# Thirty rows of one block's load moved to GpSimd's queue, over fifteen of the sixteen DMA engines

## The chip, the cores and the metric

The kernel runs on one core of one Trainium2 chip. The time is the device time of one execution in microseconds (us), the median of several runs; the span, a little shorter, is from the first to the last instruction of the profiled run. For a program on one core, a run over 1.5% above the fastest of its own kernel counts as slow.

## The reference

```python
# x: 16 x 2048 x 256, W: 256 x 256, lora_A: 256 x 16, lora_B: 16 x 256, m: 256, all float32
W_adapted = W + scale * (lora_A @ lora_B)
W_norm = np.sqrt(np.sum(W_adapted ** 2, axis=0, keepdims=True) + 1e-8)
W_final = W_adapted / W_norm * m
y = x.reshape(-1, 256) @ W_final
```

33.5 MB of x are read and 33.5 MB of y written; the weights are small.

## The kernel before

x is cut into 8 blocks of 4 MB. A block is a tile of 128 partitions with 32 KB ("a row") each. SyncE issues all loads, ScalarE all stores, each over all 128 partitions. Five block buffers hold x, and the result y is written back over it, so the load of block b + 5 waits for the store of block b. Only the last block is loaded and stored in two parts.

```python
XBUFS = 5
parts = [(b * CH, CH) for b in range(NBLK - 1)]
parts += [(NCH - CH, CH // 2), (NCH - CH // 2, CH // 2)]

def in_dram(dram, g0, cnt):
    return dram[g0 * J * P : (g0 + cnt) * J * P].rearrange("(p j) k -> p j k", p=P)

def load_x(n):
    nc.sync.dma_start(
        out=in_sbuf(*parts[n]), in_=in_dram(x_flat, *parts[n])
    ).then_inc(sem(f"load{n}"), 16)
# ... (W on SyncE; A, B and m on ScalarE)
for n in range(len(parts)):
    b = parts[n][0] // CH
    if b >= XBUFS and parts[n][0] % CH == 0:
        nc.sync.wait_ge(sem(f"store{b - XBUFS}"), 16)
    load_x(n)
# ... GpSimd, for every pair p of 4 KB column groups:
    if p == 0 or part_of[2 * p - 1] != part_of[2 * p]:
        nc.gpsimd.wait_ge(sem(f"load{part_of[2 * p]}"), 16)
    nc.gpsimd.tensor_copy(out=xb_bufs[p % NXB][:], in_=x_bufs[...])   # to bf16
# ... TensorE transposes and multiplies, VectorE and ScalarE empty PSUM, ScalarE stores
```

## Time and profile before

| | before |
|---|---|
| time, median of 3 runs | 164.03 us (163.66 to 164.14) |
| span of the profiled run | 163.2 us |
| bytes moved, mean rate | 67.41 MB, 413 GB/s |
| packets of 32 KB (one row) | 1.213 us each, load or store |
| ends of the last store on the 16 DMA engines | 159.8 to 160.7 us for fifteen, 163.2 for one |

### The profile page before, as it was taken

The numbers are of one execution on the slowest core, as the hardware profiler recorded it, in microseconds if no ns is written. First come the engines' busy times: TensorE is split into PE (matmuls) and PEld (weight loads), VectorE is DVE, ScalarE is ACT, GpSimd is POOL, SyncE is SP. The second block draws the span as 40 slices with busy tenths as digits, with TensorE's granted clock in tenths as the row PEclk, the third lists the DMA queues.
The fourth block names the chain that finished last, engine by engine and source line by source line (L and its number), as shares of the span: only waits on it lengthen the run. The fifth ranks groups of instructions, "written<-read, shape, count | busy, mean of one in ns | idle before, by whom it ended". The sixth has DMA issues, their size and how long they took to land. (4 is left out here: it accounts for less than half of the span.)

```text
span 163.2 us, 1988 instructions
## 1 busy us (share of the span) xinstructions
PE 105.3 (65%) x786; PEld 85.2 (52%) x786; DVE 47.2 (29%) x44; ACT 63.8 (39%) x67; POOL 62.5 (38%) x39
## 2 busy tenths in 40 slices
PE   1270599789789897898981998619988820892000
PEld 0130577677577775776760867418676610771000
DVE  0429452350532514405230325005051400330000
ACT  3010027548366384473754053900738440062000
POOL 1006381753935738268004940069209003900000
PEclk9999999999999999999998589985899996599755
DMA  5998998998999999999999999999999999998991
GB/s 201 402 498 386 426 474 385 482 418 265 466 426 426 442 410 466 426 394 482 418 426 442 420 426 458 402 458 410 446 414 454 414 446 422 450 442 377 442 430 60
DMA packets 2915, 67.41 MB, mean 413 GB/s; under 512 B 465, under 2 KB 482, under 8 KB 610
## 3 DMA queue, kind: packets, MB, share of 16 engines
q1 hardware_dynamic: 1440, 33.82, 49.0%
q10 hardware_dynamic: 1474, 33.59, 47.8%
q14 instruction: 1, 0.01, 0.0%
HBM read 33.85 MB, written 33.55 MB: 413 GB/s over the span
## 5 line engine op out<-in xcount | busy, mean ns | idle before, releaser
L219 ACT COPY x_sb<-y_ps 128x1024 f32<-128x1024 f32 x64 | 61.9, 1014 | 75.8 <-PE y_ps L281 75.8
L165 POOL CAST xb<-x_sb 128x2048 bf16<-128x2048 f32 x32 | 60.0, 1902 | 79.3 <-DMA x_sb<-in_x_dram 56.0
L281 PE MATMUL y_ps<-w_final,xt 128*128 128x256 bf16 x512 | 64.6, 280 | 12.8 <-PEq L256 12.8
L202 DVE COPY xt<-xt_ps 128x1024 f32<-128x1024 f32 x32 | 38.2, 1221 | 88.1 <-PE xt_ps L267 88.0
L281 PEld LDWEIGHTS y_ps<-w_final,xt 128*128 128x128 bf16 x512 | 48.4, 100 | 28.2 <-issue 19.8
L267 PE MATMUL xt_ps<-identity,xb 128*128 128x128 f32 x264 | 39.1, 309 | 23.1 <-PEq L256 23.1
L267 PEld LDWEIGHTS xt_ps<-identity,xb 128*128 128x128 f32 x264 | 34.9, 161 | 25.8 <-issue 25.6
L198 DVE TENSOR_TENSOR w_final<-wam,rnorm 128x256 bf16<-128x256 f32 x2 | 4.0, 2028 | 0.0
L244 PE MATMUL y_ps<-sq,ones 128*128 128x256 f32 x4 | 2.1, 674 | 1.6 <-DVE sq L187 1.6
L233 PE MATMUL y_ps<-identity,a_nat 128*16 128x128 f32 x2 | 0.6, 397 | 3.6 <-DMA a_nat<-in_lora_A_dram 3.6
L212 ACT ACTIVATE norm<-y_ps,eps_col 128x256 f32<-128x256 f32 x1 | 0.5, 473 | 6.1 <-PE y_ps L244 6.1
L244 PEld LDWEIGHTS y_ps<-sq,ones 128*128 128x128 f32 x4 | 1.2, 323 | 2.3 <-DVE sq L187 2.1
L210 ACT ACT_TABLE_LOAD x1 | 1.3, 1283 | 2.4 <-issue 2.4
L233 PEld LDWEIGHTS y_ps<-identity,a_nat 128*16 128x16 f32 x2 | 0.1, 90 | 3.6 <-issue 3.6
L171 POOL MEMSET xb<- 128x2048 bf16 x1 | 1.8, 1805 | 0.3 <-PE xt_ps L267 0.3
L195 DVE RECIPROCAL rnorm<-norm 128x256 f32<-128x256 f32 x1 | 1.7, 1745 | 0.0
L237 PE MATMUL y_ps<-b_bf,aT 16*128 16x256 bf16 x2 | 0.6, 404 | 1.5 <-DVE aT L180 1.5
L189 DVE COPY m_all<-y_ps 128x256 f32<-128x256 f32 x1 | 0.4, 425 | 3.3 <-PE y_ps L249 3.3
L178 DVE CAST b_bf<-b_nat 16x256 bf16<-16x256 f32 x1 | 0.3, 281 | 3.8 <-DMA b_nat<-in_lora_B_dram 3.8
L249 PE MATMUL y_ps<-m_row,ones 1*128 1x256 f32 x2 | 1.2, 710 | 0.0
L237 PEld LDWEIGHTS y_ps<-b_bf,aT 16*128 16x128 bf16 x2 | 0.1, 106 | 1.9 <-DVE aT L180 1.9
L183 DVE SCALAR_TENSOR_TENSOR wa<-y_ps,w_nat 128x512 f32<-128x512 f32 x1 | 0.7, 692 | 0.8 <-PE y_ps L237 0.8
(13 smaller groups left out, 3.7 us busy)
## 6 DMA issues: line engine op xcount, KB each, us to landing
x_sb<-in_x_dram SPq DMA_DIRECT2D x7, 4096.0 KB, 27.1
out_dram<-x_sb ACTq DMA_DIRECT2D x7, 4096.0 KB, 37.2
x_sb<-in_x_dram SPq DMA_DIRECT2D x2, 2048.0 KB, 29.6
out_dram<-x_sb ACTq DMA_DIRECT2D x2, 2048.0 KB, 20.2
w_nat<-in_W_dram SPq DMA_DIRECT2D x1, 256.0 KB, 2.9
a_nat<-in_lora_A_dram ACTq DMA_DIRECT2D x1, 16.0 KB, 2.6
b_nat<-in_lora_B_dram ACTq DMA_DIRECT2D x1, 16.0 KB, 3.6
m_row<-in_m_dram ACTq DMA_DIRECT2D x1, 1.0 KB
```

The costliest lines, as they stand in the source:

```text
L165: nc.gpsimd.tensor_copy(out=xb_bufs[p % NXB][:], in_=x_bufs[b % XBUFS][:, 2 * c * J : 2 * (c + 1) * J, :],).then_inc(sem("rounded"), 1)
L171: nc.gpsimd.memset(xb_bufs[NPR % NXB][:], 0.0).then_inc(sem("rounded"), 1)
L183: nc.vector.scalar_tensor_tensor(out=wa[:], in0=ab_ps, scalar=float(scale), in1=w_nat[:], op0=ALU.mult, op1=ALU.add).then_inc(dv, 1)
L195: nc.vector.reciprocal(out=rnorm[:], in_=norm[:]).then_inc(dv, 1)
L198: i = nc.vector.tensor_mul(out=w_final[:, t], in0=wam[:, t], in1=rnorm[:])
L202: nc.vector.tensor_copy(out=xt_bufs[p % NXT][:].rearrange("p r t -> p (r t)").bitcast(FP32), in_=xt_ps[p % 2][:],).then_inc(sem("copied"), 1)
L210: nc.scalar.activation(out=warm[:], in_=eps_col[:], func=AF.Sqrt)
L219: nc.scalar.copy(out=x_bufs[b % XBUFS][:, c * J : (c + 1) * J, :], in_=y_ps[g % 2][:]).then_inc(sem("room"), 1)
L244: i = nc.tensor.matmul(n2_ps, ones[:], sq[:, t, :], start=(t == 0), stop=(t == KC - 1))
L249: nc.tensor.matmul(mb_ps, ones[0:1, :], m_row[:], start=True, stop=True).then_inc(pe, 1)
L267: i = nc.tensor.transpose(xt_ps[p % 2][:, j * P : (j + 1) * P], xb_bufs[p % NXB][:, j, :].bitcast(FP32), identity[:],)
L281: i = nc.tensor.matmul(y_ps[h][:, j, :], xt_bufs[p % NXT][:, r : r + P, t], w_final[:, t, :], start=(t == 0 and (j % (J // 2)) == 0), stop ...
```

## The change

One of the sixteen DMA engines ends 2.5 us after the rest (marks at 160.7 and 163.2 us). The change wants to take two rows of 32 KB off it. It puts 30 rows on GpSimd's queue, means them for fifteen engines, and sends six rows of B ahead of them so that the one left out is the slow one (`SLOW = 5`). Rows 30 and 31 of block 1 go out from SyncE in pieces of 1 KB, the other 96 as one transfer.

```diff
+    SLOW = 5
+    SIDE = 30
+    n_side = next(n for n, (g0, _) in enumerate(parts) if g0 == CH)     # block 1
+    def by_gpsimd(out, in_, name, size):
+        nc.gpsimd.dma_start(
+            out=out, in_=in_, max_dma_last_dim=size, single_packet=True
+        ).then_inc(sem(name), 16)
+
+    def side_loads():
+        dst, src = in_sbuf(CH, CH), in_dram(x_flat, CH, CH)
+        half = DJ * IN * 2
+        by_gpsimd(b_nat[0 : SLOW + 1], lora_B[0 : SLOW + 1], "load_b0", OUT * 2)
+        by_gpsimd(dst[0:SIDE], src[0:SIDE], "side", half)
+        by_gpsimd(b_nat[SLOW + 1 : R], lora_B[SLOW + 1 : R], "load_b1", OUT * 2)
+
     def load_x(n):
+        dst, src = in_sbuf(*parts[n]), in_dram(x_flat, *parts[n])
+        p0 = 0
+        if n == n_side:
+            for p0 in range(SIDE, 32):
+                for s in range(2):
+                    nc.sync.dma_start(
+                        out=dst[p0 : p0 + 1].rearrange("p (j s) k -> p s j k", s=2)[:, s],
+                        in_=src[p0 : p0 + 1].rearrange("p (j s) k -> p s j k", s=2)[:, s],
+                    ).then_inc(sem(f"rows{p0}_{s}"), 16)
+            p0 = 32
+        nc.sync.dma_start(out=dst[p0:P], in_=src[p0:P]).then_inc(sem(f"load{n}"), 16)
...
-    nc.scalar.dma_start(out=b_nat[:], in_=lora_B).then_inc(sem("load_b"), 16)
...
+    side_loads()                       # ahead of GpSimd's first memset
```

(Cut: GpSimd's waits for the five parts of block 1, and VectorE's for the two parts of B.)

More of the change, by code (lines that the diff above doesn't have):

```diff
@@ L120, in in_dram, with wait_x @@
         return dram[g0 * J * P : (g0 + cnt) * J * P].rearrange("(p j) k -> p j k", p=P)
-    def load_x(n):
-        nc.sync.dma_start(
-            out=in_sbuf(*parts[n]), in_=in_dram(x_flat, *parts[n])
-        ).then_inc(sem(f"load{n}"), 16)
+    SLOW = 5
+    SIDE = 30
+    n_side = next(n for n, (g0, _) in enumerate(parts) if g0 == CH)
+    assert parts[n_side] == (CH, CH)
+    def by_gpsimd(out, in_, name, size):
[8 more added lines that the diff above has]
+        by_gpsimd(b_nat[SLOW + 1 : R], lora_B[SLOW + 1 : R], "load_b1", OUT * 2)
+    def load_x(n):
+        dst, src = in_sbuf(*parts[n]), in_dram(x_flat, *parts[n])
[9 more added lines that the diff above has]
+        nc.sync.dma_start(out=dst[p0:P], in_=src[p0:P]).then_inc(sem(f"load{n}"), 16)
+    def wait_x(n):
+        nc.gpsimd.wait_ge(sem(f"load{n}"), 16)
+        if n == n_side:
+            nc.gpsimd.wait_ge(sem("side"), 16)
+            for p0 in range(SIDE, 32):
+                for s in range(2):
+                    nc.gpsimd.wait_ge(sem(f"rows{p0}_{s}"), 16)
     def store_y(n):
@@ L161 @@
         if p == 0 or part_of[2 * p - 1] != part_of[2 * p]:
-            nc.gpsimd.wait_ge(sem(f"load{part_of[2 * p]}"), 16)
+            wait_x(part_of[2 * p])
         if p >= NXB:
@@ L176 @@
     nc.vector.memset(eps_col[:], 1e-8).then_inc(dv, 1)
-    nc.vector.wait_ge(sem("load_b"), 16)
+    nc.vector.wait_ge(sem("load_b0"), 16)
+    nc.vector.wait_ge(sem("load_b1"), 16)
     nc.vector.tensor_copy(out=b_bf[:], in_=b_nat[:])
```

## The prediction

> **What bounds the kernel now.** I read the page's slices first, then windows over the end of the span, then the chain that ended last, then SyncE's waits, and last the head.
>
> ```profile
> DMA  5998998998999999999999999999999999998991
> GB/s 201 402 498 386 426 474 385 482 418 265 466 426 426 442 410 466 426 394 482 418 426 442 420 426 458 402 458 410 446 414 454 414 446 422 450 442 377 442 430 60
> ...
> q1 hardware_dynamic: 1440, 33.82, 49.0%
> q10 hardware_dynamic: 1474, 33.59, 47.8%
> ```
>
> The 16 DMA engines are full from the second slice to the last but one: loads (q1) and stores (q10) take 49.0 + 47.8 = 97% of 16 engines' span. TensorE is busy 65% of it. So bytes over engines set the time: 67.41 MB / 16 = 4.21 MB per engine. The trace's packet records give 1.213 us for nearly every packet of 32 KB, one row of x, load or store: 27.0 GB/s per engine. 4.21 MB / 27.0 = 156 us, and the first packet starts at 2.0 us. That explains 158 us; two things explain the rest. At 36 to 38 us, when the first store joins the loads, some 26 load packets take 1.5 to 2.9 us (together 21 us over 16 engines, so 1.3 us each). The other is the end:
>
> ```profile
> 149.00:159.00 10.00, 0.00 (x0) 0.00 (x0) 0.00 (x0) 0.00 (x0) 0.00 (x0) 0.71 0.97 416
> 159.00:161.00 2.00, 0.00 (x0) 0.00 (x0) 0.00 (x0) 0.00 (x0) 0.00 (x0) 0.50 0.31 131
> 161.00:163.20 2.20, 0.00 (x0) 0.00 (x0) 0.00 (x0) 0.00 (x0) 0.00 (x0) 0.50 0.03 15
> ```
>
> These are the last windows; the last two columns are DMA share and GB/s, all engines before them idle. From 159 on the share falls to 0.31, then to 0.03, half of one engine in sixteen: one DMA engine alone works on. The completion marks of the last store say it exactly: fifteen of sixteen come between 159.8 and 160.7 us, the last at 163.2. The lateness of the last mark grows: 0.0 us at the loads of blocks 0 to 2, 0.5 at the first store, then 0.8, 1.2, 1.4, 2.0, 2.0, 2.4, 2.5, 2.5 at the eight that follow. Its cause shows too: after 45 us, about 45 packets in one unbroken series, nearly all stores, take some 1.26 us in place of 1.213, together about 2 us. So one engine is some 4% slower at storing, and it ends alone. No view names its number; the change says 5.
>
> ```profile
> 4 pieces in order of time: start us, us, what
> 145.05 0.04 issue
> 145.09 1.05 PE y_ps L281 x8
> 146.14 0.02 issue
> 146.17 1.93 ACT x_sb L219 x2
> ...
> 148.20 0.34 ACTq L128 DMA_DIRECT2D out_dram<-x_sb  x1
> ...
> SPq L123 <- DMA out_dram<-x_sb: 95.5, 3, 56.8
> ```
>
> The chain is short, and its end at 148.1 us isn't what ends the kernel: the last store is issued at 148.2, but the store before it lands only at 158.3, so the queue has 10 us of work ahead. SyncE waits for stores before loads 5 to 7 (95.5 us), but harmlessly: store 0 lands at 60.6 and load 4, still under way, at 68.1, a margin of 7.5 us; the next two margins are 7.4 us each (80.3 against 87.7, 100.0 against 107.4). Compute is hidden.
>
> [...]
>
> **The change part by part.** Block 1 has 128 rows of 32 KB, 8 per engine, 9.70 us of each.
>
> Removed from the slow engine: its 2 of the 30 rows, 2 x 1.213 = 2.43 us. Rows 30 and 31 go out as four transfers of 16 pieces of 1 KB, 4 pieces per engine. A 1 KB packet took 0.046 us in the loads of B, so +0.18 us on every engine. The other 96 rows are 6 per engine, so fifteen engines have 2 + 6 rows as before plus 0.18. B's 1 KB rows cost nothing either way.
>
> Slow engine: 163.2 - 2.43 + 0.18 = 160.95. The others: 160.7 + 0.18 = 160.9. The two meet, as if 30 rows were chosen for it. If nothing else moves: -2.25 us of span, and 164.03 - 2.25 = 161.8 us.
>
> Added: four DMA issues on SyncE (0.33 to 0.48 us each in the trace, so up to 1.9 us before load 1 is issued; load 0 occupies the engines to 13.8, hidden), five more semaphore waits on GpSimd, once, and three issues on GpSimd ahead of the identity. The head:
>
> ```profile
> 5.00 0.28 DVE L178 CAST b_bf<-b_nat 16x256 bf16<-16x256 f32 x1 [3.79 <-DMA b_nat<-in_lora_B_dram]
> ...
> 13.83 3.92 POOL L165 CAST xb<-x_sb 128x2048 bf16<-128x2048 f32 x2 [12.15 <-DMA x_sb<-in_x_dram]
> 14.05 3.98 DVE L198 TENSOR_TENSOR w_final<-wam,rnorm 128x256 bf16<-128x256 f32 x2
> 18.30 3.27 PEld L267 LDWEIGHTS xt_ps<-identity,xb 128*128 128x128 f32 x16 [7.92 <-issue]
> ```
>
> The identity (ready at 1.7, used at 3.6) may come some 3 us later, and B with it, so the weights move from 18.0 towards 20. Load 0 lands later too, as 2 rows per engine go beside it: 13.8 + 2.4 = 16.2. But w_final's two multiplications take 2.03 us each beside GpSimd's casts, where the same shape in wam took 0.76 for both; with casts from 16.2 on they may run free. The first store, issued at 34.5, moves by -0.5 to +3 us. Against the margins of 7.4 and 10 us that costs nothing.
>
> Sum: -2.43 + 0.18 + 0 for the head = -2.25 us.
>
> **The rivals.** (1) [...] Against: [...] so exact a choice of rows looks measured. I give it one in four, and half its size as likely as the whole. (2) The wrong engine is spared[...]. Then the slow one gets +0.18: 164.2 us. About one in six. (3) The lateness belongs partly to profiling: the profiled run took 164.71, timed ones 164.03. Then less than 2.25 is there to win, perhaps 1.5: 162.5 us. [...]
>
> **Range and chances.** Clean working gives 161.8; (3) and (4) pull it up by some tenths, (2) and (1) each put weight at 164 to 166. I place the middle at 162.3, and the range from 160.9 (the stall at 36 us shrinks too) to 165.2. Faster by over 2% needs under 160.75, that is 1 us beyond all that the late engine costs: 0.05. Slower by over 2%, over 167.3[...]: 0.04. The rest, 0.91.
>
> **What would show it.** Right: the window between the fifteenth and the sixteenth mark of the last store shrinks from 2.5 us to under 0.5, the DMA share falls from 0.97 to 0 within 1 us, load packets before 36 us stay at 1.213, and load 1 has one engine ahead of the rest. Wrong by (1): load packets of 1.6 to 2.4 us before 25 us, and several late engines in place of one. Wrong by (2): the last mark is again 2.5 us behind. The head is wrong if the first store is issued after 40 us or the DMA share dips after 50. A time under 160.75 would mean that the slow engine held up others as well.

The sum came to -2.25 us, so 161.8 us. Rival (1), by which the split transfers slow one another, put the time at 165.6 to 166.5 us (3.9 to 4.8 us more on the span). Rival (4): a cost of GpSimd's queue outside the span. The counts of rows per engine (8, 6 and 2) are the division of rows by engines.

## More of the kernel before

One more view is wanted for comparison: busy time by stretches, in the stage in which loads run alone (to about 36 us) and after it. A line is the stretch, its length, then busy us (and instructions) of PE, PEld, DVE, ACT and POOL, the granted TensorE clock, the mean busy share of the DMA engines, and GB/s.

```profile
8.00:22.00 14.00, 6.77 (x24) 4.96 (x25) 8.05 (x7) 0.47 (x1) 5.59 (x3) 1.00 1.04 449
22.00:36.00 14.00, 11.99 (x98) 9.82 (x97) 5.30 (x5) 7.71 (x8) 7.50 (x5) 1.00 0.96 412
40.00:60.00 20.00, 16.98 (x148) 14.27 (x147) 7.07 (x6) 11.74 (x14) 11.20 (x6) 1.00 0.99 428
```

Read the last two numbers together: the share is near 1 and the rate is 412 to 449 GB/s.

## The result

| | before | after |
|---|---|---|
| time, median | 164.05 us (4 runs) | 177.41 us (4 runs, 176.57 to 178.38) |
| ratio of the fast runs | | 1.082 (1.076 to 1.088) |
| span of the profiled run | 163.2 us | 175.6 us |

Ratios here and below are the mean time of one kernel's fast runs over that of the other's in the same rounds, so not quite the ratio of the medians. The change costs 8%, and the prediction's range (160.9 to 165.2) missed it by 12 us.

The page's slices of the changed kernel, each 4.4 us, and its new queue:

```profile
DMA  5999969999999999999999999899998999999993
GB/s 191 423 280 255 233 142 224 239 336 388 463 440 403 455 396 455 455 396 455 440 403 470 388 448 465 381 429 448 422 470 384 466 455 388 455 448 396 416 425 131
...
q0 software_dynamic: 144, 1.00, 2.1%
```

The DMA engines still look full in every slice. But from the third to the eighth the rate falls to 142 to 280 GB/s, where it was 385 to 498 before. The same in stretches, as above:

```profile
4.00:8.00 4.00, 0.59 (x2) 0.11 (x2) 0.00 (x0) 0.00 (x0) 0.18 (x1) 1.00 0.92 395
8.00:22.00 14.00, 0.00 (x0) 0.00 (x0) 0.00 (x0) 0.00 (x0) 0.00 (x0) 1.00 1.13 263
22.00:36.00 14.00, 4.01 (x9) 2.01 (x10) 7.01 (x10) 0.47 (x1) 3.79 (x2) 1.00 0.90 194
40.00:60.00 20.00, 16.98 (x148) 14.27 (x146) 7.59 (x7) 11.56 (x12) 11.31 (x7) 1.00 1.01 436
```

Between 8 and 22 us the share is 1.13 (a packet counts in the stretch in which it starts, so it can pass 1) and the rate 263; from 22 to 36, 0.90 and 194. Busy engines that move half the bytes have packets that last twice as long, and the trace's packet records say so: the 96 rows of block 1's rest take 2.67 us on average, none under 1.59, against 1.213. From 40 us on, both kernels move 428 to 436 GB/s: the damage is done in the pure load stage and never regained.

I added up, over all packets, what each took beyond the usual (1.213 us for 32 KB, 0.611 for 16 KB and so on) and divided by 16: the excess per engine. Up to 45 us it is 14.2 us after and 1.5 before, a difference of 12.7 us. The last data packet ends at 175.1 against 162.7 us, 12.4 later. So the stretched packets account for the whole loss. The 14.2 us split into 8.7 us in the 96 rows, 3.2 in block 0, about half of which runs beside the 30 rows, 1.3 in the 30 rows themselves, 0.2 in the 1 KB pieces, and 0.8 in what comes next.

Two more differences catch the eye. The first is the head:

```profile
23.97 3.79 POOL L202 CAST xb<-x_sb 128x2048 bf16<-128x2048 f32 x2 [19.79 <-DMA x_sb<-in_x_dram]
24.31 1.69 DVE L216 CAST b_bf<-b_nat 16x256 bf16<-16x256 f32 x1 [23.09 <-DMA b_nat<-in_lora_B_dram]
...
51.26 0.37 ACTq L165 DMA_DIRECT2D out_dram<-x_sb  x1
```

The second part of B lands only behind the 30 rows (at 24.2 us, they at 23.6), so its cast waits until 24.3 us (5.0 before), and the first store goes out at 51.3 in place of 34.5. Whether those 17 us count is tested below. The second is the end:

```profile
160.00:171.00 11.00, 0.00 (x0) 0.00 (x0) 0.00 (x0) 0.00 (x0) 0.00 (x0) 0.58 0.99 425
171.00:173.00 2.00, 0.00 (x0) 0.00 (x0) 0.00 (x0) 0.00 (x0) 0.00 (x0) 0.50 0.69 295
173.00:175.60 2.60, 0.00 (x0) 0.00 (x0) 0.00 (x0) 0.00 (x0) 0.00 (x0) 0.50 0.04 19
```

There is again one engine alone in the last 2 us (0.04 of sixteen). The completion marks of the last store (sixteen, read here as one per DMA engine, which fits that share): one engine at 171.4, fourteen from 172.8 to 173.9, one at 175.6. One engine was indeed spared, and leads: at the load of the 96 rows already one mark comes at 34.4 us and the others from 36.9 to 38.3, about two rows of 1.213 us later. But another is late.

### The profile page after: what moved, and what is told of

Same layout as the page of the kernel before. It is cut to its first block, busy times and chain, and to the rows that moved or that the text cites. A ratio compares the mean times of both kernels' runs of the same rounds, so it can differ in the third digit from the quotient of the medians.

```text
span 175.6 us, 1997 instructions
## 1 busy us (share of the span) xinstructions
PE 100.9 (57%) x786; PEld 82.5 (47%) x786; DVE 45.3 (26%) x44; ACT 63.6 (36%) x67; POOL 64.2 (37%) x42
## 5 line engine op out<-in xcount | busy, mean ns | idle before, releaser
L319 PE MATMUL y_ps<-w_final,xt 128*128 128x256 bf16 x512 | 62.1, 273 | 13.4 <-PEq L294 13.4
L319 PEld LDWEIGHTS y_ps<-w_final,xt 128*128 128x128 bf16 x512 | 47.2, 98 | 27.4 <-issue 20.1
L305 PE MATMUL xt_ps<-identity,xb 128*128 128x128 f32 x264 | 37.0, 299 | 17.9 <-PEq L294 17.9
L305 PEld LDWEIGHTS xt_ps<-identity,xb 128*128 128x128 f32 x264 | 33.4, 156 | 20.2 <-issue 20.1
L216 DVE CAST b_bf<-b_nat 16x256 bf16<-16x256 f32 x1 | 1.7, 1686 | 23.1 <-DMA b_nat<-in_lora_B_dram 23.1
L131 POOL DMA_DIRECT2D b_nat<-in_lora_B_dram x2 | 1.3, 626 | 1.1 <-SPq L58 1.1
```

What stands on the lines that cost most here:

```text
L131: nc.gpsimd.dma_start(out=out, in_=in_, max_dma_last_dim=size, single_packet=True).then_inc(sem(name), 16)
L216: nc.vector.tensor_copy(out=b_bf[:], in_=b_nat[:])
L305: i = nc.tensor.transpose(xt_ps[p % 2][:, j * P : (j + 1) * P], xb_bufs[p % NXB][:, j, :].bitcast(FP32), identity[:],)
L319: i = nc.tensor.matmul(y_ps[h][:, j, :], xt_bufs[p % NXT][:, r : r + P, t], w_final[:, t, :], start=(t == 0 and (j % (J // 2)) == 0), stop ...
```

## The experiments

Theories: **P**, a transfer over only part of the 128 partitions has longer packets by itself, on whatever queue it goes (its half rate was the author's estimate); **Q**, GpSimd's queue itself slows packets; **D**, the DRAM side does; **late weights**, the delayed compute costs; **wrong engine**, the spared one isn't the slow one. Each run's packets were read from its trace. All results were correct except where said.

### Which of the parts stretches the packets

**Block 1 in two halves by SyncE, nothing on GpSimd's queue** (e1_halves).

```diff
+        if n == 1:
+            nc.sync.dma_start(out=dst[0:64], in_=src[0:64]).then_inc(sem("half0"), 16)
+            nc.sync.dma_start(out=dst[64:P], in_=src[64:P]).then_inc(sem("load1"), 16)
```

> Block 1 loaded by SyncE as two transfers, of partitions 0 to 63 and 64 to 127, nothing else changed and nothing on GpSimd's queue. Theory P [...] the 32 KB load packets of block 1 take about 2.43 us in place of 1.213, 8 x 1.21 = 9.7 us more, time about 173 to 174 us. Theory Q (the software queue of GpSimd is what slows the packets): no change, 164 us.

Measured: 173.7 us, ratio 1.063 (1.060 to 1.065). Stretches of the trace, block 1 being loaded from 13 to 34 us:

```profile
8.00:22.00 14.00, 7.79 (x37) 5.58 (x35) 6.06 (x8) 1.45 (x3) 7.47 (x4) 1.00 1.05 300
22.00:36.00 14.00, 7.55 (x64) 6.12 (x64) 2.36 (x2) 6.74 (x8) 1.79 (x1) 0.92 1.01 260
```

The shares are 1.05 and 1.01, the rates 300 and 260. The packets of block 1 have a median of 2.56 us. Simply cutting a 128-partition load into two halves costs 10 us, and GpSimd's queue has no part in it. That is what P expects.

**The whole of block 1 on GpSimd's queue** (e3_block_gpsimd).

```diff
+    nc.gpsimd.dma_start(
+        out=in_sbuf(*parts[1]), in_=in_dram(x_flat, *parts[1]),
+        max_dma_last_dim=DJ * IN * 2, single_packet=True,
+    ).then_inc(sem("load1"), 16)
```

> The whole of block 1, all 128 partitions in one transfer, goes out on GpSimd's queue in pieces of 16 KB; nothing else changed. Theory P: [...] packets of 16 KB take 0.611 us and of 32 KB 1.213 us, and the time is 164 us plus or minus 1. Theory Q: packets on GpSimd's queue, and those beside them, take up to twice that, and the time rises by some 5 to 10 us.

Measured: 163.67 us, ratio 1.000 (0.998 to 1.002). The same stretches:

```profile
8.00:22.00 14.00, 4.15 (x14) 2.52 (x13) 3.61 (x6) 0.47 (x1) 3.73 (x2) 1.00 1.04 448
22.00:36.00 14.00, 11.48 (x89) 9.35 (x88) 4.81 (x4) 7.71 (x8) 5.69 (x4) 1.00 0.97 419
```

They are those of the kernel before, with 256 packets of 16 KB on GpSimd's queue at 0.611 us. Q is out: with all 128 partitions in the transfer, the queue cost nothing here.

**The 30 rows on SyncE, too** (e2_side_sync).

```diff
-        by_gpsimd(dst[0:SIDE], src[0:SIDE], "side", half)
+            nc.sync.dma_start(out=dst[0:SIDE], in_=src[0:SIDE]).then_inc(sem("side"), 16)
```

> The changed kernel, but the 30 rows go out on SyncE's queue behind block 0 [...]; only B's two transfers stay on GpSimd. Theory P: block 0 loads at full speed (1.213 us packets), then the 30 rows and the 96 rows both run at about half rate, 128 rows x 1.21 / 16 = 9.7 us lost: about 172 to 176 us. Theory Q: packets at 1.213, about 164 us.

Measured: 177.82 us, ratio 1.086. Block 0, now alone, is back at 1.234 us a row; the 30 rows take 2.34 and the 96 rows 2.65, as P expects. The excess is 11.9 us, 2.4 less than the change's 14.2, yet the time is no better, and 2 us above the band that P gave. The end of the trace shows why:

```profile
162.00:166.00 4.00, 4.00 (x25) 3.40 (x24) 2.45 (x2) 0.65 (x1) 1.80 (x1) 0.65 0.75 320
166.00:169.00 3.00, 2.68 (x25) 2.23 (x24) 0.00 (x0) 2.70 (x4) 0.00 (x0) 1.00 0.03 11
169.00:176.00 7.00, 0.34 (x4) 0.10 (x1) 0.00 (x0) 0.51 (x1) 0.00 (x0) 0.69 0.71 301
```

From 166 to 169 us the DMA engines are idle (share 0.03). B lands early here, so the first store goes out at 37.0 us, and stores share the engines with loads for longer; the last load lands only at 158.1 (148.4 in the change), and its result, 11 us later, finds the store queue empty. The engines idle for some 4.7 us each ahead of the last 6 us of the run. So the change's late weights seem to have had a side that helped.

**Halves again, filled with other rows of DRAM** (h1_halves_other_rows, shown against e1_halves; wrong: relative error 0.50).

```diff
-            nc.sync.dma_start(out=dst[0:64], in_=src[0:64])...
-            nc.sync.dma_start(out=dst[64:P], in_=src[64:P])...
+            nc.sync.dma_start(out=dst[0:64], in_=src[0:P:2])...
+            nc.sync.dma_start(out=dst[64:P], in_=src[1:P:2])...
```

> As e1_halves, but the lower 64 partitions are filled with every second row of block 1 in DRAM, from all of its 4 MB, and the upper 64 with the others; the result is wrong on purpose (rows of block 1 change places). Theory P[...]: packets of block 1 still take about 2.5 us, time 173 to 175 us. Theory D (it is the DRAM side: a transfer of 64 rows reads 2 MB in place of 4, and sixteen engines collide there): packets fall to about 1.2 us, time 164 us.

Measured: 173.77 us, ratio 1.060 (1.056 to 1.064).

```profile
8.00:22.00 14.00, 7.09 (x34) 5.08 (x33) 6.06 (x8) 0.79 (x2) 6.60 (x4) 1.00 1.05 300
22.00:36.00 14.00, 8.07 (x69) 6.34 (x67) 2.36 (x2) 7.39 (x8) 2.05 (x2) 0.92 0.98 243
```

The packets again have a median of 2.56 us, though each transfer now reads from the block's whole 4 MB. D is out in this form: packets stretch wherever the rows come from, once block 1 goes out in transfers over part of the 128 partitions.

What it is about such transfers that stretches packets stays open. Every slow stretch held a transfer over fewer than 128 partitions, and no run separates "one half" from "fewer partitions": a transfer over 64 partitions taken from both halves (32 to 95) was not tried, and the 96 rows, which lie in both halves, are as slow (2.67 us) as the halves (2.56). So that partial transfers cost the time is shown; why, is not.

**Halves where stores run beside the load** (f3_halves_block5): the edit of e1_halves with 5 for 1.

> As e1_halves, but the block that is split into partitions 0 to 63 and 64 to 127 is block 5, which is loaded while stores run. Theory P1[...]: load packets of block 5 stretch little, the time rises by 0 to 3 us: 164 to 167 us. Theory P2[...]: 32 KB load packets of 2.4 us again for block 5, and the time rises by 5 to 10 us as in e1_halves.

Measured: 171.43 us, ratio 1.047 (1.044 to 1.050). First the kernel before, then this one, in the stretch in which block 5 is loaded:

```profile
68.00:96.00 28.00, 21.46 (x162) 17.47 (x160) 8.88 (x8) 12.28 (x13) 14.94 (x8) 0.88 1.01 434
```

```profile
68.00:96.00 28.00, 15.25 (x128) 12.30 (x128) 5.71 (x5) 11.57 (x12) 7.46 (x4) 0.90 1.00 314
```

The rate falls from 434 to 314 GB/s at a full share. Load packets take 2.00 us on average, and the store packets beside them 1.36 in place of 1.213. P2 is the nearer one: the later place saves only a quarter of the loss (7.7 us of excess, against 10.7 in e1_halves). So moving the 30 rows to a later block would hardly have saved the change.

**No 1 KB pieces: 32 rows on GpSimd's queue, with no engine meant to be spared** (g4_no_short_rows): `SIDE = 32`. Theory A: the split itself makes nearly all of the loss; theory B: the pieces of 1 KB do.

> The change with 32 rows on GpSimd's queue[...] and so without the four transfers of 1 KB pieces; the 96 rows as in the change. Theory A[...]: mean of the 96 rows' packets still 2.4 us or more, time within 2 us of the change, 175 to 178 us. Theory B[...]: packets of the 96 rows at 1.2 to 1.6 us, time 166 to 170.

Measured: 174.11 us, ratio 1.063 (1.058 to 1.068).

```profile
8.00:22.00 14.00, 0.00 (x0) 0.00 (x0) 0.00 (x0) 0.00 (x0) 1.92 (x2) 1.00 1.08 300
22.00:36.00 14.00, 6.06 (x19) 4.06 (x20) 7.07 (x11) 0.47 (x1) 2.04 (x2) 1.00 0.96 246
```

The rates, 300 and 246, are still far under the 449 and 412 of before, and the 96 rows take 2.37 us a packet: A, but for its bands, which were a little too high (by 1 us in the time). The excess is 10.8 us, 3.4 less than the change's, of which 1.7 in the 96 rows and 1.0 in block 0. It seems that the pieces of 1 KB, counted in the prediction at 0.18 us, cost more through what they hold up: in the change the first packets of the 96 rows, right behind them, take up to 4.6 us; here none takes over 2.57. But this run also has 32 rows in place of 30 on GpSimd's queue, so the two aren't separated.

### Whether the late weights cost

**B on ScalarE's queue as before** (g3_b_early): the two loads of B on GpSimd's queue go, the old one on ScalarE's comes back.

> The change with B loaded as in the kernel before, on ScalarE's queue, and only the 30 rows on GpSimd's. B then lands at 4 to 5 us, not 23.6, and the first store can go out at about 37 in place of 51 us. Theory A (the late weights are off the path, as the DMA engines are full all the same): the time doesn't fall; it may even rise by 0 to 3 us, as stores that start early take turns from the loads and the last load comes later: 176 to 180 us. Theory B (the late start of compute is what costs): the time falls by several us, to 165 to 172.

Measured: 176.29 us, ratio 1.073. The first store goes out at 42.3 us (37 had been expected), 9 us earlier than in the change, and little is won: the mean of its four runs, 176.0, lies 1.5 us under that of the change's two fast runs of the same rounds (below), which themselves lie 2.1 us apart. The excess is 13.5 us, and some 2.0 us of idle per engine appear near the end, as in e2_side_sync. Theory B, with 165 to 172 us, is out; the late weights are nearly or wholly hidden behind full DMA engines (shares of 1.05 from 8 to 22 us and 1.00 from 22 to 36).

### Which engine is slow, and which was spared

No view names DMA engines, so I built a ladder: extra loads of 15, 14, ... 1 rows. It numbers the engines by an assumption of mine, that row r of every such load goes to one and the same engine, called r; then a late mark that goes away between e + 1 and e rows belongs to engine e. Of this, f1 below shows only that a load of k rows has k marks and that one late mark is there down to 5 rows and gone at 4.

**Behind load 5** (e4_ladder):

```diff
+        if b == XBUFS:
+            for k in range(15, 0, -1):
+                nc.sync.dma_start(out=scratch[at : at + k], in_=x_flat[0 : 8 * k]...)
```

> The kernel before, plus fifteen small loads of 15, 14, ... 1 rows of 8 KB into a scratch tile, issued by SyncE behind load 5. [...] engine e gets 15 - e extra packets of about 0.31 us: a ladder of extra work from 4.6 us on engine 0 to none on engine 15. Theory A (engine 5 is the slow one): the last mark of the last store comes at 163.2 + 10 x 0.31 = 166.3 us, about 1 us after the mark of engine 0 at 160.5 + 4.6 = 165.1, and the rung of engine 5 (163.6) is missing among the others. Theory B (another engine e is the slow one): the last or late mark lies at 163.2 + (15 - e) x 0.31, and rung e is missing.

Measured: 177.09 us, ratio 1.082: a miss, useless for the purpose. The rungs (one rung is one of these loads) came 1.5 to 2.8 us apart (marks from 92 to 126 us), and the loads behind them piled up: load 6's marks spread from 109.7 to 136.0 us. As an estimate from the packets' times, that is one or two store packets of 32 KB before each row of 8 KB (1.213 + 0.309 = 1.5 us, 2 x 1.213 + 0.309 = 2.7 us).

The same trace holds a limit of P. Thirteen of the first rung's packets, 8 KB each and all to partitions 0 to 14, are in flight together from 90.44 to 90.49 us, and each takes 0.309 us, as every rung's packets do on the median. So thirteen packets at one moment to so few partitions didn't stretch rows of 8 KB; the stretch is shown in unbroken series, for pieces of 16 KB (0.96 us on average for the 30 rows of the change, against 0.611) and rows of 32 KB (2.67 for the 96, against 1.213). From what length on it sets in, no run shows.

**Behind the last load** (f1_ladder_tail): the same with rows of 10 KB, where nothing waits for it.

> Fifteen extra loads of 15, 14, ... 1 rows of 10 KB into a scratch tile, now issued by SyncE behind the last load, so that nothing waits for them; they run beside the last stores. [...] the k marks of one rung come from engines with equal work, but for the slow engine, whose mark is 1.5 to 2.5 us late in every rung with k above its number and missing below. Theory A (engine 5 is slow): the late mark is there in the rungs of 15 to 6 rows and gone in those of 5 to 1. Theory B (another engine e): it goes away between e+1 and e rows. The kernel ends with engine 0, about 15 x 0.38 = 5.7 us behind the fifteen engines of before: 166 to 168 us of span.

Measured: one look, 169.0 us (a single run, so of unknown state). The completion marks of some rungs, in us, as read from the trace:

```
rows   marks
10     152.5 152.5 153.0 153.1 153.1 153.2 153.3 153.6 153.7   154.6
 7     157.0 157.3 157.4 157.6 157.7 158.0                     159.3
 6     158.6 158.9 159.0 159.2 159.6                           160.9
 5     159.6 160.1 160.4 160.7                                 161.9
 4     161.2 161.5 161.8 162.2
 3     162.8 163.1 163.8
 2     164.4 165.4
```

One mark comes 0.9 to 1.3 us behind the others in every rung down to 5 rows and is gone at 4. (At 2 rows the marks lie 1.0 us apart too, so ordinary scatter can be nearly as large; g2 below tests the reading.) In the ladder's numbering the slow engine is 4, theory B with e = 4, not 5.

**With B in 6 and 10 rows and one row of 64 KB on GpSimd's queue between** (f2_ladder_cursor).

> The same ladder, with B loaded on GpSimd's queue in 6 and 10 rows as in the change, and between the two, in the place of the 30 rows, one row of 64 KB copied from DRAM to DRAM[...]. Theory A[...]: a second late mark is there in the rungs of 15 to 7 rows and gone from 6 on; so the 30 rows of the change left out engine 5. Theory B[...]: the second late mark goes away at another rung, or all marks are late by a little if the row is split over several engines.

Measured: one look, 169.01 us. The 64 KB went out as 16 packets of 4 KB and gave no second late mark: inconclusive on which engine the change left out, by my choice of transfer. The one late mark again goes away between 5 and 4 rows (161.2 us, 0.9 behind the others, at 5; no gap at 4).

**The change again, and with a lead of 5 and 11 rows** (g1_change_again, g2_lead_of_5).

```diff
-    SLOW = 5
+    SLOW = 4
```

> The changed kernel itself, again, beside its variants on one chip. Expected: 176.5 to 178.5 us as before, load packets of about 2x before 37 us, one DMA engine some 1.4 us ahead of the rest at the last store and another some 2 us behind.

> The change with B led by 5 and 11 rows in place of 6 and 10[...]. The ladder put the slow engine at number 4. Theory A (the change spared the wrong engine by one): now the slow engine is the spared one, the gap between the fifteenth and the last mark of the last store falls from about 1.7 us to under 0.7, no engine is 1 us ahead at the end, and the time is 1 to 2 us below the change's, about 175.5 us; the 2x load packets stay. Theory B[...]: the gap and the time stay within 0.5 us of the change's.

Measured: the change again 178.54 and 176.48 us in its two fast runs, two more at 179.5 and 179.7 counted as slow, so without a ratio; one engine 2.0 us ahead of the next at the last store and one 1.7 behind, as expected. With the lead of 5, 175.95, 175.39 and 175.74 in the fast runs (one slow of 181.05), ratio to before 1.071 (1.065 to 1.077). The end of its trace:

```profile
160.00:172.00 12.00, 0.00 (x0) 0.00 (x0) 0.00 (x0) 0.00 (x0) 0.00 (x0) 0.65 0.97 414
172.00:173.00 1.00, 0.00 (x0) 0.00 (x0) 0.00 (x0) 0.00 (x0) 0.00 (x0) 0.50 0.88 377
173.00:174.30 1.30, 0.00 (x0) 0.00 (x0) 0.00 (x0) 0.00 (x0) 0.00 (x0) 0.50 0.07 25
```

The share goes from 0.88 to 0.07 with no lone engine behind it; all sixteen marks lie between 173.3 and 174.3 us, and none leads. Against the change's two profiles, 175.6 and 177.0, that is 1.3 us and more; the fast runs' means, 175.7 and 177.5, differ by 1.8. Theory A, on one profile: with one row less in the lead the spared engine is the slow one, so, as far as the marks show, the sparing works as it was meant to, and the change aimed it one engine too far. (This chip is another than the ladders'.) But its whole worth, near 2 us, is a sixth of what the split costs.

No version tried beats the kernel before; the best of them, the whole block on GpSimd's queue, equals it. As an estimate from these runs, sparing by this form of split can't pay: it spares 2.43 us of one engine, and the 96 rows alone cost every engine 7 to 8.7 us.

## Why the prediction was wrong, point by point

- **What bounds the kernel**: right. The DMA engines set the time in every run, but for some idle near the end of three (4.7 us per engine in e2, 2.0 in g3, 1.0 in e1); the packets' excess (12.7 us) explains the loss (12.4).
- **The step that failed**: "The other 96 rows are 6 per engine, so fifteen engines have 2 + 6 rows as before plus 0.18." The count of rows was kept and the time per row taken over with it. A row of the 96 took 2.67 us, not 1.213, and one of block 0, in part beside the 30 rows, 1.61 on average. The term given as +0.18 us was 12.7, so "-2.43 + 0.18 + 0 for the head = -2.25 us" turned into a loss.
- **Rival (1), that the split transfers slow one another**: what happened (e1, e3, h1; halves and mere fewer partitions aren't separated), with one chance in four and at 3.9 to 4.8 us. The working of its size left some engines near 1.213 us; none of the 96 rows' packets took under 1.59, and the excess was 12.7 us. How rows are dealt out, no run shows.
- **The argument against it**, that "so exact a choice of rows looks measured", judged the author and not the machine. It should have had no weight: no trace spoke for it, and the trace of before, in which all big transfers have 128 partitions, couldn't rule the rival out.
- **Rival (2), the wrong engine**: also true, by one place in the ladder's numbering (f1, g2). It costs about 2 us of the 13. The text took the change's word for the number.
- **Rivals (3) and (4)** ((4), a cost of GpSimd's queue): e3 shows no such cost (ratio 1.000), and g2 closes the gap at the end nearly wholly in its profile. What part of the gap profiling makes stays open.
- **The head**: "may come some 3 us later" was wrong by a wide margin (B's second part came at 24.2 us, as it queued behind the 30 rows, and block 0 at 23.9, not 16.2), but the conclusion, that it costs nothing, stood to within 1.5 us (g3).
- **The 0.04 for "slower by over 2%"**: it took rival (1) at its full size as the worst case, and that size was about a third of the excess measured (3.9 to 4.8 against 12.7 us).

## What to carry to other kernels

A partial transfer's time here wasn't its bytes over sixteen engines: ask over how many partitions it runs, and what runs beside it. Where all DMA engines are full, keep loads at all 128 partitions, since halves (2.56 us a packet), or a 30 + 96 split (2.67 us for the 96), ran at about half the rate of whole blocks (1.213 us) here, and before any delicate balancing test its carrier alone. A DMA share near 1 proves nothing about the rate (1.05 at 300 GB/s in e1_halves, 1.04 at 449 before); read GB/s beside it.

## What the runs leave open

- How the rows of a partial transfer are dealt to engines, and why their packets last longer.
- Why one engine is slower on stores: some 1.26 us in place of 1.213, in the kernel before, which has no transfer on GpSimd's queue.
- The stall of the kernel before at 36 to 38 us, some 26 load packets of 1.5 to 2.9 us (1.5 us per engine in all excess before 45 us; 1.1 in e3_block_gpsimd). Its cause stays open.
